# The feed-forward part of an encoder layer in two halves of channels, with a token-stationary up projection

## The chip, the cores and the metric

The kernel runs on one core of one Trainium2 chip. The metric is the device time of one execution in microseconds: 1326.75 us as the median of three runs of the kernel before. A core has five engines that run side by side and wait for each other through semaphores: TensorE (PE, matrix products), VectorE (DVE), ScalarE (ACT), GpSimd (POOL) and SyncE (SP, which issues most transfers). Matrix products write into eight banks of PSUM, from which DVE and ACT fetch them.

## The reference

One layer over 256 tokens of width 2048: a token mixer, then the part that is changed here, a convolutional gated MLP with 5504 channels, then a last norm. All inputs are float32.

```python
def conv_ffn(x, g_norm, w_up, conv_k, conv_b, w_down):
    h = rms_norm(x, g_norm)
    up = h @ w_up                                  # (256, 2048) @ (2048, 11008)
    t = up.shape[1]
    pad = jnp.pad(up, ((0, 0), (1, 1), (0, 0)))
    up = (pad[:, :t] * conv_k[0] + pad[:, 1:t + 1] * conv_k[1]
          + pad[:, 2:t + 2] * conv_k[2] + conv_b)  # width 3, over the tokens
    gate, val = jnp.split(up, 2, axis=-1)
    return x + (jax.nn.silu(gate) * val) @ w_down  # (256, 5504) @ (5504, 2048)
```

## The kernel before

Every product of two float32 matrices is done as three products of a rounded type: each operand is split into a high part and a low part, and high x high, low x high and high x low are added up in PSUM. Weights come from memory in pieces (tile `wraw`, five buffers). ACT writes the high part of a piece (`whi`, line 142), DVE the low part (`wlo`, line 143), both with four buffers. The function `begin(i)`, called ahead of piece i's products, issues the loads five pieces ahead, emits the split three pieces ahead, and then runs the tasks that other functions have hung on this step with `at(i, f)`. The program is emitted in exactly this order, and each engine works through its own list in order: what stands behind a waiting instruction waits as well. In the text a step is such an i.

There are two ways to multiply. In the weight-stationary one (`stationary`, `spread_products`, lines 194 and 198) a 128 x 128 block of weights is the stationary operand. The high part of the weights meets 512 columns, 256 tokens of the high and 256 of the low activations, and the low part of the weights meets the 256 high ones. In the token-stationary one (`wide`, `run_wide`, `triple`, lines 272 to 274) 128 tokens are stationary and 512 columns of weights move; one row block k of the weights, 2 x 512 columns wide, takes four triples of products (two token halves, two column halves). There, two neighbouring row blocks (a tile pair, a "quad" in the code) can be multiplied as a 2 x 2 block product with seven triples in place of eight. For this DVE forms sums of the activations (`act_sums`, lines 279 to 291, with a high part on ACT) and sums of the weights (`weight_sums`, lines 297 to 300; high and low parts in lines 307 and 308), and at the end sums of the results. In its own step i a tile pair has its activation sums made at i - 5 and i - 4, its weight sums at i - 3 and their parts at i - 2.

The feed-forward part before: the up projection is weight-stationary, in 22 groups of two channel blocks (the last of one) for gate and value each. After a group ACT and DVE add the two column halves (lines 936 and 938), multiply by the reciprocal of the norm (`rb`, line 944), convolve with three taps (lines 946 to 951), gate (lines 956 and 957) and split the result into `a` (lines 467 and 468). All 43 channel blocks are kept in SBUF. Then the down projection is token-stationary in two passes of 43 row blocks and 1024 columns each, with seven tile pairs in each pass:

```python
DOWN_QUADS = ((4, 6, 9, 11, 14, 16, 18), (3, 5, 8, 10, 13, 15, 17))
```

Its first pass is added to the residual `x2` while the second runs (`ev_down`, line 971); the second ends column half by column half (`finish`), with the last norm and the output.

## Time and profile before

| | |
|---|---|
| runs | 1326.64, 1326.75, 1327.16 us |
| profiled execution | 1326.71 us, span of its instructions 1324.7 us |
| TensorE busy | 1312.2 us (99%), granted clock 0.998 |
| VectorE busy | 1033.1 us (78%) |
| ScalarE busy | 763.7 us (58%) |
| up projection on TensorE | 605.74 to 1090.32 us of the span |
| down projection on TensorE | 1090.32 to about 1315.4 us |
| memory traffic | 253.90 MB read, 193 GB/s over the span |

The page lists each engine's busy time and the chain of work that ended last. The trace behind it also answers with lists of instructions in order of time (start, duration, engine, line, operation, tiles, count), with busy times of chosen stretches, with groups of equal instructions, and with sums of waits. In a product's name the moving operand stands first and the stationary one second. Durations of products overlap, so the pace of a stream is the distance between starts. Where several equal instructions are merged into a row, its duration runs from the first's start to the last's end.

### The profile page before, as it was taken

To read this page: it belongs to the slowest core of one execution; us is meant where nothing else is said; L and a number is where in the kernel's file an instruction comes from. 1 tells how busy PE (TensorE), PEld (TensorE's weight loads), DVE (VectorE), ACT (ScalarE), POOL (GpSimd) and SP (SyncE) were. 2 spreads that over 40 slices of the span, in tenths; PEclk is the share of its full clock that TensorE was granted. 3 is DMA by queue.
4 is the path that set the end of the run, shared out by engine and by line. 5 is a ranking of instruction groups with operands and counts; after the bars stand their busy time and mean duration, and the time that the engine had idled before them with its cause. 6 is when DMAs were issued, how large, how long until landed. Compare 5 with 4: busy or idle time off the path is not lost.

```text
span 1324.7 us, 19275 instructions
## 1 busy us (share of the span) xinstructions
PE 1312.2 (99%) x6791; PEld 1113.9 (84%) x6791; DVE 1033.1 (78%) x1561; ACT 763.7 (58%) x1127; POOL 105.0 (8%) x192
## 2 busy tenths in 40 slices
PE   9999999999999999999999999999999999999997
PEld 7888888888887888888888888888888888888885
DVE  6477667767598966986777778787878779999997
ACT  6665566667554644556655555565656556555553
POOL 0251145530000000000000000000000000000000
PEclk9999999999999999999999999999999999999999
DMA  9765785654656666665566665666666656656653
GB/s 329 228 182 182 212 225 171 210 175 154 198 173 209 202 195 224 218 208 175 175 192 190 182 194 183 190 182 192 183 191 191 191 148 234 215 192 207 213 197 121
DMA packets 174800, 259.37 MB, mean 196 GB/s; under 512 B 12920, under 2 KB 124400, under 8 KB 174704
## 3 DMA queue, kind: packets, MB, share of 16 engines
q1 hardware_dynamic: 170416, 250.31, 59.5%
q0 software_dynamic: 3968, 7.30, 2.2%
q8 instruction: 53, 0.87, 0.3%
q10 hardware_dynamic: 320, 0.53, 0.1%
q14 instruction: 43, 0.35, 0.1%
HBM read 253.90 MB, written 2.10 MB: 193 GB/s over the span
## 4 chain that ended last, share of the span: by engine, by line
PE 98%; DVE 1%; DMA 0%; ACT 0%; issue 0%; SPq 0%; ACTq 0%; DVEq 0%
PE bank L194 31%; PE bank L198 16%; PE bank L274 10%; PE bank L272 10%; PE bank L273 10%; PE bank L215 7%; PE bank L216 7%; PE bank L217 7%; PE bank L710 1%; DMA wraw<-in_w_in_dram 0%; PE bank L760 0%; PE bank L586 0%; PE bank L921 0%; PE bank L750 0%; PE bank L485 0%
## 5 line engine op out<-in xcount | busy, mean ns | idle before, releaser
L143 DVE TENSOR_TENSOR wlo<-wraw,whi 128x1024 fp32r<-128x1024 f32 (+1 forms) x471 | 554.2, 1186 | 216.9 <-ACT whi L142 205.4
L142 ACT ACTIVATE whi<-wraw 128x1024 fp32r<-128x1024 f32 (+1 forms) x471 | 477.3, 1026 | 297.3 <-PE bank L194 114.1
L194 PE MATMUL bank<-h,whi 128*128 128x512 f32 x1760 | 479.5, 395 | 0.0
L194 PEld LDWEIGHTS bank<-h,whi 128*128 128x128 f32 x1760 | 301.9, 189 | 41.5
L198 PEld LDWEIGHTS bank<-h,wlo 128*128 128x128 f32 x1760 | 267.3, 189 | 35.6
L198 PE MATMUL bank<-h,wlo 128*128 128x256 f32 x1760 | 276.7, 281 | 0.0
L215 PE MATMUL bank<-whi,h 128*128 128x512 f32 x256 | 102.2, 399 | 0.2 <-ACT whi L142 0.2
L274 PE MATMUL bank<-wlo,a 128*128 128x512 f32 x260 | 101.4, 390 | 0.2 <-DVE wlo L143 0.2
L272 PE MATMUL bank<-whi,a 128*128 128x512 f32 x260 | 101.2, 389 | 0.0
L273 PE MATMUL bank<-whi,a 128*128 128x512 f32 x260 | 101.2, 389 | 0.0
L216 PE MATMUL bank<-whi,h 128*128 128x512 f32 x256 | 100.1, 391 | 0.6 <-DVE h L464 0.6
L217 PE MATMUL bank<-wlo,h 128*128 128x512 f32 x256 | 100.1, 391 | 0.0
L946 ACT ACTIVATE tc<-ta,ck 128x256 f32<-128x256 f32 x86 | 47.3, 597 | 69.8 <-DVE ta L944 69.8
L274 PEld LDWEIGHTS bank<-wlo,a 128*128 128x128 f32 x260 | 48.8, 188 | 11.0 <-DVE wlo L143 1.0
L1222 POOL DMA_DIRECT2D gfin<-in_norm_final_dram x4 | 2.2, 550 | 700.2 <-DVE tc L957 580.4
L272 PEld LDWEIGHTS bank<-whi,a 128*128 128x128 f32 x260 | 48.8, 188 | 10.1
L273 PEld LDWEIGHTS bank<-whi,a 128*128 128x128 f32 x260 | 48.8, 188 | 10.1
L216 PEld LDWEIGHTS bank<-whi,h 128*128 128x128 f32 x256 | 48.1, 188 | 10.7 <-DVE h L464 1.4
L217 PEld LDWEIGHTS bank<-wlo,h 128*128 128x128 f32 x256 | 48.0, 188 | 10.7 <-DVE wlo L143 0.4
L215 PEld LDWEIGHTS bank<-whi,h 128*128 128x128 f32 x256 | 48.1, 188 | 10.1 <-ACT whi L142 0.6
L949 DVE SCALAR_TENSOR_TENSOR tc<-ta,ck,tc 128x255 f32<-128x255 f32 x86 | 41.4, 482 | 14.5 <-ACT tc L946 14.5
L215 PE MATMUL bank<-whi,y 128*128 128x512 f32 x128 | 50.4, 394 | 0.0
(254 smaller groups left out, 1684.8 us busy)
## 6 DMA issues: line engine op xcount, KB each, us to landing
wraw<-in_w_up_dram SPq DMA_DIRECT2D x336, 256.0 KB, 3.2
wraw<-in_w_in_dram SPq DMA_DIRECT2D x111, 512.0 KB, 4.0
wraw<-in_w_down_dram SPq DMA_DIRECT2D x86, 512.0 KB, 4.7
wraw<-in_w_in_dram SPq DMA_DIRECT2D x66, 256.0 KB, 3.8
wraw<-in_w_branch_dram SPq DMA_DIRECT2D x32, 512.0 KB, 3.8
wraw<-in_w_out_dram SPq DMA_DIRECT2D x32, 512.0 KB, 3.7
xs<-in_x_dram SPq DMA_DIRECT2D x8, 256.0 KB, 7.3
vw<-va POOLq DMA_DIRECT2D x32, 64.0 KB, 4.9
```

The costliest lines, as they stand in the source:

```text
L142: nc.scalar.activation(h[:, k, :m], w[:, k, :m], AF.Copy)
L143: nc.vector.tensor_sub(l[:, k, :m], w[:, k, :m], h[:, k, :m].bitcast(F32))
L194: nc.tensor.matmul(p, h[:, k - k0, b * 128:(b + 1) * 128], acts(k), start=k == 0, stop=k == nk - 1)
L198: nc.tensor.matmul(p[:, :T], l[:, k - k0, b * 128:(b + 1) * 128], acts(k)[:, 0, :], start=False, stop=False)
L215: nc.tensor.matmul(p, xh, h[:, kk, :m], start=st, stop=False)
L216: nc.tensor.matmul(p, xl, h[:, kk, :m], start=False, stop=False)
L217: nc.tensor.matmul(p, xh, l[:, kk, :m], start=False, stop=sp)
L272: nc.tensor.matmul(p, xh, h, start=st, stop=False)
L273: nc.tensor.matmul(p, xl, h, start=False, stop=False)
L274: nc.tensor.matmul(p, xh, l, start=False, stop=sp)
L946: nc.scalar.activation(v, u, AF.Identity, scale=ck[:, 1, ch:ch + 1], bias=ck[:, 3, ch:ch + 1])
L949: nc.vector.scalar_tensor_tensor(v[:, 1:], u[:, :T - 1], ck[:, 0, ch:ch + 1], v[:, 1:], op0=OP.mult, op1=OP.add)
```

## The change

The 43 channel blocks are cut into a first half of 20 and a second of 23. Each half does its up projection and then its share of the down projection, so that the down projection has four passes: two of 20 row blocks and two of 23. The first three are added to the residual from PSUM (`ev_part`, `ev_down`), the last ends as before.

The up projection becomes token-stationary, in groups of four channel blocks (the last of three) for gate and value: a piece of weights is one row block of 2 x 512 columns, gate and value, in one transfer. Pairs 3 and 5 of the eight row block pairs of a group are done with seven block products, except in the last group. The activations' sums for these two pairs are made once and used by all groups. The result now has tokens on the partitions. It is gathered in two tiles, `xa` and `xb` (first the sums of the seven products, then the plain products are added), and each channel block is then turned on TensorE: a product of 128 x 128 with the block as stationary operand and, as moving operand, a diagonal matrix with the reciprocal norm of the tokens (`rb`), for gate and value and both token halves. ACT copies the turned block from PSUM (`u`, three buffers). The multiplication by the norm on DVE goes. The taps, the gate and the split of a block are now spread over five steps (`conv`). The tiles for the sums lie in a pool of their own, since the activations `h` must last until the second half. The tile pairs of the down projection are 2 and 3 in the first half, 3 and 4 in the second.

```diff
@@ -45,7 +45,12 @@
 OUT_QUADS = ((3, 5), (1, 3))
 OUT_ORDER = (tuple(range(16)), (0, 1, 6, 7, 2, 3, 10, 11, 4, 5, 8, 9, 12, 13, 14, 15))
 TURN_X2 = (13, 1)
-DOWN_QUADS = ((4, 6, 9, 11, 14, 16, 18), (3, 5, 8, 10, 13, 15, 17))
+FFN_CUT = 20
+UP_QUADS = (3, 5)
+UP_TURN = (2, 3, 4, 5)
+UP_CONV = ((4, 7, 10, 13), (4, 6, 8, 10))
+DOWN_QUADS = (((5, 7), (2, 4, 6)), ((5, 7, 9), (2, 4, 6, 8)))
+ROOM_OF = {"f": "t13", "s": "xb"}
 
 
 @with_exitstack
...
-    def wide(src, row0, order, c0, acts, quads, room, done, sums=None):
-        n0 = plan_wide(src, row0, order, c0)
+    def wide(src, row0, order, c0, acts, quads, room, done, sums, pair=None, cn=512, step=512):
+        n0 = plan_wide(src, row0, order, c0, cn, step)
...
-                sum_acts_at(i - 5, i - 4, b["acts"], lambda k=order[2 * q]: ff["ap"][k // 2], room, "s")
+                sum_acts_at(i - 5, i - 4, b["acts"], lambda k=order[2 * q]: pair(k // 2), room, "s")
...
-            triple(C[t][c], x_of(order[i - n0], t), h[:, c], l[:, c], i == n0, i == n1 - 1)
+            triple(C[t][c][:, :cn], x_of(order[i - n0], t), h[:, c, :cn], l[:, c, :cn], i == n0, i == n1 - 1)
...
         s = const.tile([128, NT], F32, name="ss2")
         nc.vector.tensor_reduce(s, rs["ss"], axis=AX.X, op=OP.add)
         r = rstd("n2", s, D, RMS_EPS)
-        at(cur[0] + 3, lambda: rs.__setitem__("rb", bcast_cols(r)))
+        d = const.tile([128, T], F32, name="rb")
+        for t in range(NT):
+            nc.vector.tensor_scalar(d[:, t * 128:(t + 1) * 128], ident, r[:, t:t + 1], None, op0=OP.mult)
+        rs["diag"] = d
 
     def turn_x2(j):
         x2 = rs["x2"]
...
                                         x2[:, t, c * 128:(c + 1) * 128], ident)
             k = j * 4 + k2 * 2
             rs["h", k], rs["h", k + 1] = new_pair(hpool, f"h{k // 2}")
+            rs["hp", k // 2] = pair_of[hpool, f"h{k // 2}"]
             split_pair(p, (rs["h", k], rs["h", k + 1]), gffn[:, k:k + 2])
 
 
     ff = {}
 
-    def ev_up(f0, nb):
+    def ffn_room(name, dt):
+        return ff["room"].tile([128, 2, 512], dt, name=ROOM_OF.get(name, name))
+
+    def up_tiles():
+        x = [ffn_room(n, F32) for n in ("xa", "xb")]
+        ff["x"] = [[x[t][:, c] for c in range(2)] for t in range(NT)]
+
+    def ev_up_sums(P, i):
+        def go():
+            up_tiles()
+            p1, p5, p6, p7 = P
+            (x11, x12), (x21, x22) = ff["x"]
+            nc.scalar.activation(x11, p1, AF.Copy)
+            nc.vector.tensor_add(junk, p6, x11)
+            nc.vector.tensor_add(x12, p5, junk)
+            nc.vector.tensor_add(x21, p7, junk)
+            nc.vector.tensor_add(x22, p5, x21)
+
+        at(i + 1, go)
+
+    def ev_up(f0, a0, nb, summed, last):
         def done(ps, i):
-            n = nb
-            a = []
-            for p in ps:
-                t = tmp.tile([128, T], F32, name="tb", bufs=3)
-                nc.scalar.activation(t, p[:, T:], AF.Copy)
-                u = tmp.tile([128, T], F32, name="ta", bufs=6)
-                nc.vector.tensor_add(u, p[:, :T], t)
-                a.append(u)
+            m = nb * 128
+            if not summed:
+                up_tiles()
+            x = ff["x"]
+            for t in range(NT):
+                for c in range(2):
+                    v = x[t][c][:, :m]
+                    if summed:
+                        nc.vector.tensor_add(v, ps[t][c], v)
+                    elif c:
+                        nc.vector.tensor_copy(v, ps[t][c][:, :m])
+                    else:
+                        nc.scalar.activation(v, ps[t][c][:, :m], AF.Copy)
+            u = {}
+
+            def turn(b):
+                p = bank()
+                for c in range(2):
+                    for t in range(NT):
+                        nc.tensor.matmul(p[:, c * T + t * 128:c * T + (t + 1) * 128],
+                                         x[t][c][:, b * 128:(b + 1) * 128],
+                                         rs["diag"][:, t * 128:(t + 1) * 128], start=True, stop=True)
+                u[b] = ff["room"].tile([128, 2, T], F32, name="u", bufs=3)
+                nc.scalar.activation(u[b].rearrange("p a b -> p (a b)"), p, AF.Copy)
 
             def conv(b):
-                c = []
-                for u, ch in ((a[b], f0 + b), (a[n + b], NF + f0 + b)):
-                    nc.vector.tensor_mul(u, u, rs["rb"])
-                    v = ff["p"].tile([128, T], F32, name="tc", bufs=4)
-                    nc.scalar.activation(v, u, AF.Identity, scale=ck[:, 1, ch:ch + 1], bias=ck[:, 3, ch:ch + 1])
-                    c.append((u, v, ch))
-                for u, v, ch in c:
-                    nc.vector.scalar_tensor_tensor(v[:, 1:], u[:, :T - 1], ck[:, 0, ch:ch + 1], v[:, 1:],
-                                                   op0=OP.mult, op1=OP.add)
-                    nc.vector.scalar_tensor_tensor(v[:, :T - 1], u[:, 1:], ck[:, 2, ch:ch + 1], v[:, :T - 1],
-                                                   op0=OP.mult, op1=OP.add)
-                at(cur[0] + 1, lambda: gate(b, c[0][1], c[1][1]))
-
-            def gate(b, g, v):
-                nc.scalar.activation(g, g, AF.Silu)
-                nc.vector.tensor_mul(g, g, v)
-                at(cur[0] + 1, lambda: split_plain(g, ff["a"][f0 + b]))
-
-            at(i + 1, lambda: conv(0))
-            if n > 1:
-                at(i + (5 if f0 + 3 == NF else 3), lambda: conv(1))
+                j = cur[0]
+                v = [tmp.tile([128, T], F32, name="ta", bufs=6) for _ in range(2)]
+                chs = [c * NF + f0 + b for c in range(2)]
+
+                def taps():
+                    for c, ch in enumerate(chs):
+                        nc.vector.scalar_tensor_tensor(v[c][:, 1:], u[b][:, c, :T - 1], ck[:, 0, ch:ch + 1], v[c][:, 1:],
+                                                       op0=OP.mult, op1=OP.add)
+                        nc.vector.scalar_tensor_tensor(v[c][:, :T - 1], u[b][:, c, 1:], ck[:, 2, ch:ch + 1],
+                                                       v[c][:, :T - 1], op0=OP.mult, op1=OP.add)
+
+                y = ff["a"][a0 + b]
+                for c, ch in enumerate(chs):
+                    nc.scalar.activation(v[c], u[b][:, c], AF.Identity, scale=ck[:, 1, ch:ch + 1],
+                                         bias=ck[:, 3, ch:ch + 1])
+                at(j + 1, taps)
+                at(j + 2, lambda: nc.scalar.activation(v[0], v[0], AF.Silu))
+                at(j + 3, lambda: nc.vector.tensor_mul(v[0], v[0], v[1]))
+                at(j + 4, lambda: nc.scalar.activation(y[:, 0, :], v[0], AF.Copy))
+                at(j + 5, lambda: nc.vector.tensor_sub(y[:, 1, :], v[0], y[:, 0, :].bitcast(F32)))
+
+            for b in range(nb):
+                at(i + UP_TURN[b], lambda b=b: turn(b))
+                at(i + UP_CONV[last][b], lambda b=b: conv(b))
         return done
...
+    def ev_part(g):
+        def done(ps, i):
+            for j in range(2):
+                for t in range(NT):
+                    add_down(ps[t][j], t, 2 * g + j)
+        return done
...
-    g_up = []
-    for f in range(0, NF, 2):
-        nb = min(2, NF - f)
-        g_up.append(stationary(w_u, 0, KD, f * 128, nb * 128, 2, DFF, lambda k: rs["h", k], ev_up(f, nb)))
-    h_room = {n: f"h{i}" for i, n in enumerate(("t13", "t24", "h13", "h24", "l13", "l24", "f", "s"))}
-
-    def down_room(name, dt):
-        return hpool.tile([128, 2, 512], dt, name=h_room[name])
-
-    g_dn = [wide(w_d, 0, range(NF), g * 1024, lambda k: ff["a"][k], DOWN_QUADS[g], down_room,
-                 (ev_sums(2 * g, down_room), ev_down if g == 0 else finish)) for g in range(2)]
+    h_sums = {2 * q: {} for q in UP_QUADS}
+    halves = []
+    for f0, f1 in ((0, FFN_CUT), (FFN_CUT, NF)):
+        ups = []
+        for f in range(f0, f1, 4):
+            nb = min(4, f1 - f)
+            quads = UP_QUADS if nb == 4 else ()
+            ups.append(wide(w_u, 0, range(KD), f * 128, lambda k: rs["h", k], quads, ffn_room,
+                            (ev_up_sums, ev_up(f, f - f0, nb, bool(quads), f + 4 >= f1)), h_sums, cn=nb * 128, step=DFF))
+        downs = [wide(w_d, f0 * 128, range(f1 - f0), g * 1024, lambda k: ff["a"][k], DOWN_QUADS[len(halves)][g], ffn_room,
+                      (ev_sums(2 * g, ffn_room), ev_part(g) if not halves else finish if g else ev_down), None,
+                      lambda q: ff["ap"][q]) for g in range(2)]
+        halves.append((f1 - f0, ups, downs))
+    for n, q in enumerate(UP_QUADS):
+        i = halves[0][1][0][1] + 1 + 3 * n
+        sum_acts_at(i, i + 1, h_sums[2 * q], lambda q=q: rs["hp", q], ffn_room, f"s{n}")
 
 
     preload[0] = [lambda: load_x(0, 256)]
...
-    for g in g_up:
-        run_group(g)
...
-    run_wide(g_dn[0])
-    run_wide(g_dn[1], SPLIT_AHEAD + 1)
...
+    for n, ups, downs in halves:
+        ff["ap"] = [fa.tile([128, min(2, n - k), 2, T], F32R, name=f"a{k // 2}") for k in range(0, n, 2)]
+        ff["a"] = [ff["ap"][k // 2][:, k % 2] for k in range(n)]
+        for g in ups:
+            run_wide(g)
+        run_wide(downs[0])
+        run_wide(downs[1], SPLIT_AHEAD + 1 if downs is halves[1][2] else 0)
```

How this moves instructions, at three places. First TensorE in the up projection, before: the end of one group of two channel blocks and the start of the next (`h_5971` and `h_5762` are pairs of activations, `whi` and `wlo` the parts of the weights).

```order
L194 MATMUL bank<-h_5971,whi 128x512 x4
L198 MATMUL bank<-h_5971,wlo 128x256 x8
L194 MATMUL bank<-h_5971,whi 128x512 x4
L194 MATMUL bank<-h_5762,whi 128x512 x4
L198 MATMUL bank<-h_5762,wlo 128x256 x4
```

There each block of weights is loaded once for a product of 512 columns and its low part once for one of 256; nothing but such products stands there.

And of the change: the end of the group's second step, a turned block, and the start of its third step.

```order
L277 MATMUL bank<-whi,h_5760 128x512
L278 MATMUL bank<-whi,h_5760 128x512
L279 MATMUL bank<-wlo,h_5760 128x512
L980 MATMUL bank<-rb,xa 128x128
L980 MATMUL bank<-rb,xb 128x128
L980 MATMUL bank<-rb,xa 128x128
L980 MATMUL bank<-rb,xb 128x128
L277 MATMUL bank<-whi,h_5770 128x512
L278 MATMUL bank<-whi,h_5770 128x512
L279 MATMUL bank<-wlo,h_5770 128x512
```

The four products of L980 are new and stand between two steps of the next group, ahead of each of its steps 2 to 5 (counted from 0); the products around them have gone from blocks of weights as stationary operand to tokens.

Second, DVE in the first pass of the down projection, before: from the activation sums of the second tile pair to the weight sums (h6 the sums, h0 and h1 the weights' sums, h7 the low part of the activation sums).

```order
L279 TENSOR_TENSOR h6_11123<-a6_5863 128x512
L281 TENSOR_TENSOR h6_11123<-h6_11123 128x128
L282 TENSOR_TENSOR h6_11123<-h6_11123 128x128
L283 TENSOR_TENSOR h6_11123<-h6_11123 128x128
L284 TENSOR_TENSOR h6_11123<-h6_11123 128x128
L143 TENSOR_TENSOR wlo_11144<-wraw_11117,whi_11143 128x1024
L291 TENSOR_TENSOR h7_11147<-h6_11123,h7_11147 128x512
L143 TENSOR_TENSOR wlo_11166<-wraw_11141,whi_11165 128x512
L297 TENSOR_TENSOR h0_11169<-wraw_11141 128x512
L298 TENSOR_TENSOR h1_11170<-wraw_11163,h0_11169 128x512
L299 TENSOR_TENSOR h0_11169<-wraw_11163,wraw_11141 128x512
L300 TENSOR_TENSOR h1_11170<-wraw_11163,h1_11170 128x512
```

What stands there is the two pairs' sums and the low parts of weights alone.

Third, the same place of the change, in the first half: from the activation sums of its second tile pair to its weight sums (`ta` are the convolved blocks, `a8` the split result, `u` the turned blocks).

```order
L1006 TENSOR_TENSOR a8_5865<-ta_7989,a8_5865 128x256
L1004 TENSOR_TENSOR ta_8056<-ta_8056,ta_8057 128x256
L993 SCALAR_TENSOR_TENSOR ta_8116<-u_7998,ck_87,ta_8116 128x255
L995 SCALAR_TENSOR_TENSOR ta_8116<-u_7998,ck_87,ta_8116 128x255
L993 SCALAR_TENSOR_TENSOR ta_8117<-u_7998,ck_87,ta_8117 128x255
L995 SCALAR_TENSOR_TENSOR ta_8117<-u_7998,ck_87,ta_8117 128x255
L148 TENSOR_TENSOR wlo_8167<-wraw_8134,whi_8166 128x1024
L296 TENSOR_TENSOR xb_8170<-t13_8140,xb_8170 128x512
L148 TENSOR_TENSOR wlo_8195<-wraw_8164,whi_8194 128x512
L302 TENSOR_TENSOR t13_8198<-wraw_8164 128x512
L303 TENSOR_TENSOR t24_8199<-wraw_8192,t13_8198 128x512
L304 TENSOR_TENSOR t13_8198<-wraw_8192,wraw_8164 128x512
```

Between the sums of the second tile pair now stand the split of one block (L1006), the gate of the next (L1004) and the taps of a third (L993 and L995), which belong to the up projection's last group.

46 lines of the change are left out of this document (18 added, 28 removed).

## The prediction

> **What bounds the kernel now.** I read the page's totals and its chain first, then what TensorE (PE) waited for, then the stages.
>
> ```profile
> PE 1312.2 (99%) x6791; PEld 1113.9 (84%) x6791; DVE 1033.1 (78%) x1561; ACT 763.7 (58%) x1127; POOL 105.0 (8%) x192
> PE 98%; DVE 1%; DMA 0%; ACT 0%; issue 0%; SPq 0%; ACTq 0%; DVEq 0%
> ```
>
> The waits of PE, longest first (total, times, longest), begin with this row, and two stretches of 45 and 22 us of the up and the down projection read so (busy PE, weight loads, DVE, ACT, POOL; granted clock; DMA share, GB/s):
>
> ```profile
> PE bank L422 <- POOL ident masks.py:199: 1.4, 1, 1.4
> ```
>
> ```profile
> 765.00:810.00 45.00, 45.00 (x258) 39.37 (x257) 34.77 (x57) 26.16 (x42) 0.00 (x0) 1.00 0.61 188
> 1228.00:1250.00 22.00, 22.00 (x99) 18.22 (x98) 21.34 (x30) 13.04 (x15) 0.00 (x0) 1.00 0.65 220
> ```
>
> The longest wait of PE in the whole span is 1.4 us, at the start. In both stretches PE never stops, at clock 1.00, so the end moves by what is added to or taken from PE's stream, as long as the others keep up. They have unequal room: DVE is busy 77% of the up stretch and 97% of the down stretch, ACT 58% and 59%.
>
> A busy PE says nothing of its pace, since recorded matmuls overlap. I therefore price by distances between starts.
>
> ```profile
> 605.74 1.07 PE L194 MATMUL bank<-h,whi 128*128 128x512 f32 x4
> ...
> 608.52 1.04 PE L921 MATMUL bank<-ident,x 128*128 128x128 f32 x8
> 609.31 1.17 PE L194 MATMUL bank<-h,whi 128*128 128x512 f32 x4
> 610.32 0.64 PE L198 MATMUL bank<-h,wlo 128*128 128x256 f32 x4
> 610.79 1.09 PE L194 MATMUL bank<-h,whi 128*128 128x512 f32 x4
> 611.72 0.64 PE L198 MATMUL bank<-h,wlo 128*128 128x256 f32 x4
> ...
> 629.91 0.61 PE L449 MATMUL bank<-ident,n_r 128*128 128x128 f32 x4
> 630.27 1.17 PE L194 MATMUL bank<-h,whi 128*128 128x512 f32 x4
> ...
> 1090.32 0.39 PE L272 MATMUL bank<-whi,a 128*128 128x512 f32 x1
> ```
>
> The up projection runs from 605.74 to 1090.32, 484.6 us. Within it stand two sets of eight transposes (L921), which stay, 0.87 us each with the slower restart behind them (609.31 - 608.52 = 0.79, then 1.01 instead of 0.93), and the broadcast of the norm (L449), 630.27 - 629.91 = 0.36 and the same slower restart, 0.44 us. The products take 484.6 - 1.7 - 0.4 = 482.4 us for 86 blocks x 16 = 1376 pairs, 0.351 us a pair. A 512-column product costs 0.93/4 = 0.232 us, a 256-column one 0.47/4 = 0.118.
>
> ```profile
> 1194.82 0.39 PE L274 MATMUL bank<-wlo,a 128*128 128x512 f32 x1
> ...
> 1209.78 0.39 PE L274 MATMUL bank<-wlo,a 128*128 128x512 f32 x1
> ```
>
> In the token-stationary form of the down projection 66 products of 512 columns lie between these starts: 14.96/66 = 0.2267 us each.
>
> **The change, part by part. Products.** A pair held 512 + 256 columns for one block and one k; in the new form eight blocks and one k are 12 products of 512 columns, the same 6144 columns. Ten groups of four channel blocks have 16 x 4 = 64 triples, less one for each of their two tile pairs: 62. That is 10 x 62 x 3 x 0.2267 = 421.7 us. The last group has three blocks, no tile pair and 64 x 3 = 192 products of 384 columns; halfway between 0.118 and 0.2267 I take 0.172, 33.0 us. Together 454.7 us, 27.7 less than 482.4: 20 x 0.68 = 13.6 from the seven block products, the other 14.1 from pace.
>
> **The turn.** Each of 43 blocks now needs four products of 128 columns, a block of sums as stationary and the diagonal with the norm as moving operand, both plain float32. The nearest rows are the gMLP's mix, which has just this form and type, and the transposes within a 512-column stream:
>
> ```profile
> L586 PE MATMUL bank<-wsT,vg x32: 271/275/275, 88.4 to 122.3; 128*128 128x128 f32 x32
> 87.93 0.63 PE L198 MATMUL bank<-h,wlo 128*128 128x256 f32 x4
> 88.40 0.61 PE L586 MATMUL bank<-wsT,vg 128*128 128x128 f32 x4
> 88.77 1.17 PE L194 MATMUL bank<-h,whi 128*128 128x512 f32 x4
> 89.77 0.64 PE L198 MATMUL bank<-h,wlo 128*128 128x256 f32 x4
> 595.79 1.03 PE L921 MATMUL bank<-ident,x 128*128 128x128 f32 x8
> 596.58 0.48 PE L272 MATMUL bank<-whi,m 128*128 128x512 f32 x1
> 596.90 0.40 PE L273 MATMUL bank<-whi,m 128*128 128x512 f32 x1
> ```
>
> The kernel writes two products per group of the mix, 16 in all; the trace holds 32. So a float32 product runs as two passes, and a turn is eight. Four passes cost 88.77 - 88.40 = 0.37 and a restart 0.07 longer; eight would be 0.37 x 2 + 0.07 = 0.81 us. The eight transposes cost 596.90 - 595.79 - 0.23 = 0.88. I take 0.88, as its neighbours are the 512-column ones: 43 x 0.88 = 37.8 us, with 34.8 as the low end. So the turn eats more than the products give.
>
> [...]
>
> **Down projection.** Fourteen tile pairs become 2 + 3 + 3 + 4 = 12: two triples more, 1.4 us. The broadcast goes: -0.4. PE's sum: -27.7 + 37.8 + 1.4 - 0.4 = +11.1 us. Against the profiled execution's 1326.71 us (span 1324.7; the median of the runs, 1326.75, is the same) this gives 1337.8.
>
> **What must hide beside it.** Per up group DVE now does the following, priced by distances between starts:
>
> ```profile
> 710.99 0.42 DVE L468 TENSOR_TENSOR a<-tc,a 128x256 fp32r<-128x256 f32 x1
> 711.32 1.22 DVE L143 TENSOR_TENSOR wlo<-wraw,whi 128x1024 fp32r<-128x1024 f32 x1
> 703.52 0.48 DVE L949 SCALAR_TENSOR_TENSOR tc<-ta,ck,tc 128x255 f32<-128x255 f32 x1 [0.34 <-ACT tc L946]
> 705.36 1.22 DVE L143 TENSOR_TENSOR wlo<-wraw,whi 128x1024 fp32r<-128x1024 f32 x1
> 1202.02 2.48 DVE L971 TENSOR_TENSOR x<-bank,x 128x512 f32<-128x512 f32 x4
> 1204.41 1.22 DVE L143 TENSOR_TENSOR wlo<-wraw,whi 128x1024 fp32r<-128x1024 f32 x1
> 1235.24 0.69 DVE L279 TENSOR_TENSOR h<-a 128x512 f32<-128x512 f32 x1
> 1236.90 1.22 DVE L143 TENSOR_TENSOR wlo<-wraw,whi 128x1024 fp32r<-128x1024 f32 x1
> 1238.04 0.69 DVE L291 TENSOR_TENSOR h<-h,h 128x512 fp32r<-128x512 f32 x1
> 1238.64 0.69 DVE L143 TENSOR_TENSOR wlo<-wraw,whi 128x512 fp32r<-128x512 f32 x1
> 1239.24 0.69 DVE L297 TENSOR_TENSOR h<-wraw 128x512 f32<-128x512 f32 x1
> 1241.78 1.22 DVE L143 TENSOR_TENSOR wlo<-wraw,whi 128x1024 fp32r<-128x1024 f32 x1
> 1242.91 2.35 DVE L308 TENSOR_TENSOR h<-h,h 128x1024 fp32r<-128x1024 f32 x2
> 1245.18 1.22 DVE L143 TENSOR_TENSOR wlo<-wraw,whi 128x1024 fp32r<-128x1024 f32 x1
> 1246.32 0.69 DVE L279 TENSOR_TENSOR h<-a 128x512 f32<-128x512 f32 x1
> ```
>
> A low part of 1024 elements takes 1.14, of 512 0.60, a 256-element operation 0.33, the four taps of a block 1.84, four additions from PSUM 2.4 (some 2.7 where one needs the last). For a tile pair: sums of the activations 1.66 and their low part 0.60, sums of the weights 2.54 and their low parts 2.27. An up group: 14 x 1.14 + 2 x 0.60 + 2 x (2.54 + 2.27) + 2.7 + 2.4 + 4 x (1.84 + 2 x 0.33) = 41.9 us, against 42.2 + 3.5 = 45.7 us of PE. That hides: at 92% DVE is below the 97% with which the down stretch ran without a PE wait. ACT's new copy of each turned block goes into its idle 42%; the four passes over the residual instead of two add 2 x 12 additions of 0.60 on DVE, 14.4 us, and the two pairs fewer take 2 x 7.1 off. The up loads become one transfer of 512 KB for two of 256 KB, at the same bytes; the 188 GB/s above carry them, and if not, DVE's low parts are late by what a transfer is.
>
> The down projection does not hide so well. A step, one row block of weights, is 12 products, 2.72 us of PE; a tile pair shortens its two steps by 0.68 together. From 1235.24 to 1246.32 the trace shows a whole period of a pair every four steps: 11.1 us of DVE against 4 x 2.72 - 0.68 = 10.2 of PE. Each such pair makes DVE 0.9 us later, and the low parts are made three steps ahead (two for a pair's second block), a cover of 5.4 us. Before, three such pairs in a row were the most, and longer gaps followed. Now runs of pairs every four steps fill both second passes, and the first pass of each half lies on the tail of the convolutions. In half one's first pass, from step 5 up to the low part that step 14 needs, DVE has six low parts of 1024 and two of 512 (8.0), for its two pairs 2 x (1.66 + 0.60 + 2.54) + 2.27 = 11.9, the taps of four blocks (7.4) and five operations of 256 (1.6): 28.9 us. PE has 9 x 2.72 - 0.68 + 0.88 = 24.7 in steps 5 to 13, and 1.1 us more in step 14 before the product that uses it: 3.1 us of waiting, with the rest of the down projection queued behind that product on PE. The same sums give, as estimates, 1.7 us for its second pass, 3.4 for the first pass of half two (three pairs, three blocks) and 5.6 for the last (four pairs, and 2.4 + 2.4 of additions and scaling). Together 13.8; for the passes before, they give none, as PE's waits show. DVE may start a pair's low part a step sooner than I count, so I take 12, between 0 and 23. Forecast: 1337.8 + 12 = **1350 us**, 1.8% slower.
>
> **The rivals.** *PE's sum alone* (DVE's lateness stays under its cover): 1338, up to 1342. For it: PE waited nowhere in the passes before, at 97% DVE. Against it: the 28.9 against 24.7.
>
> *DVE bounds the up groups too.* Then the recorded durations, not the distances, count:
>
> ```profile
> L143 DVE TENSOR_TENSOR wlo<-wraw,whi 128x1024 fp32r<-128x1024 f32 x437 | 531.2, 1225 | 208.4 <-ACT whi L142 200.2 <-PE bank L849 3.0 <-DMA wraw<-in_w_in_dram 2.3
> ```
>
> By them (1.225 here; 0.69 for 512 elements, 0.48 a tap and 0.42 for 256 in the rows above) a group is 45.5 us, level with PE, and any wait on ACT is lost: at step 5 the fourth turned block's copy on ACT must wait for the first one's taps, since there are three buffers, and the next high part stands behind it, some 1.6 us. Ten groups: +16, 1366. Against it: in the rows above the next operation starts 0.09 us before the recorded end. [...]
>
> *The turn is cheap*, the other sign: its weight loads run under the preceding 512-column products, and only columns count. From 0.2267 and 0.118, a column costs 0.000425 us and 128 of them, with the same fixed part, 0.064: 344 passes x 0.064 = 22.0 us, 15.8 less. Without DVE waits 1322, faster by 0.4%; it decides below 0.078 us a pass, where 344 passes take less than 37.8 - 11.1 = 26.7 us. Against it: eight transposes in that very stream cost 0.11 each.
>
> *The seven-product form brings nothing* because its sums come late: at step 6 their low parts, made at step 4, have 3 steps' cover against 3.4 us of DVE work. It would return 13.6 us and end at 1363; I count it to the second rival.
>
> **Numbers.** Forecast with DVE late in the down passes 54%, PE's sum alone 27%, DVE bound throughout 10%, cheap turn 6%, and 3% for a cheap turn paid back by waits, near no change. The last two leave faster at 6%, within 0.2% (what a measurement here can tell from none) 3%, slower 91%. The range from 1337 to 1361 holds the first two cases whole; its ends are the sum with no wait and with some 23 us.
>
> **What would show it.** Right: L980 with 344 records at about 0.11 us a pass; up groups of 45.7 us on PE; waits of PE on DVE's low part (L148) only in the four down passes, 2 to 6 us in each, the last the longest. Wrong: passes under 0.08 us, PE waits within up groups, or none at all. A time under 1330 would overthrow the price of the turn, one above 1363 the DVE distances.

## The result, and the profile after

The changed kernel takes 1361.49 us (median of four runs, 1361.00 to 1361.69) against 1326.72 us (1326.64 to 1327.16) for the kernel before on the same chip: a ratio of 1.0261, 95% interval 1.0243 to 1.0279. The forecast of 1350 us had the sign right and was 11.5 us short; the time lies 0.5 us above the range. The profiled execution has a span of 1359.9 us.

The totals and the chain of the page after:

```profile
PE 1333.7 (98%) x6437; PEld 1118.1 (82%) x6437; DVE 1107.5 (81%) x1605; ACT 784.8 (58%) x1133; POOL 103.8 (8%) x190
PE 89%; DVE 8%; issue 1%; ACT 1%; DMA 0%; DVEq 0%; ACTq 0%
```

The chain was 98% PE and 1% DVE before; DVE's 8% are new. Stretches after: about one up group, most of the first pass of the down projection, then the middle of its third pass and most of its last (length; busy PE, weight loads, DVE, ACT, POOL; granted clock; DMA share, GB/s):

```profile
748.00:794.00 46.00, 46.00 (x223) 38.70 (x222) 41.94 (x61) 28.28 (x41) 0.00 (x0) 1.00 0.58 183
834.00:890.00 56.00, 50.17 (x228) 40.92 (x227) 47.55 (x76) 30.90 (x46) 0.00 (x0) 0.97 0.47 159
1250.00:1282.00 32.00, 29.13 (x120) 23.31 (x119) 31.72 (x46) 16.80 (x21) 0.00 (x0) 0.95 0.55 182
1282.00:1345.00 63.00, 57.63 (x241) 46.67 (x241) 61.54 (x91) 33.34 (x44) 0.00 (x0) 0.95 0.41 142
```

In the up group PE never stops. In the third and the last down pass DVE is busy 99 and 98% (31.72 of 32, 61.54 of 63) and PE 91%; in the first pass DVE has gaps (47.55 of 56, 85%), and still PE stands at 90%. Before, PE stood at 100% in the stretch shown of the down projection. The mean granted clock of these stretches falls to 0.95 to 0.97.

The turn and the group in the order of time on PE: a turn with its neighbours, then the first product behind the first turn of three successive groups.

```profile
655.57 0.38 PE L980 MATMUL bank<-rb,xa 128*128 128x128 f32 x2
...
656.37 0.48 PE L277 MATMUL bank<-whi,h 128*128 128x512 f32 x1
656.69 0.40 PE L278 MATMUL bank<-whi,h 128*128 128x512 f32 x1
...
702.62 0.48 PE L277 MATMUL bank<-whi,h 128*128 128x512 f32 x1
...
748.43 0.48 PE L277 MATMUL bank<-whi,h 128*128 128x512 f32 x1
...
794.21 0.48 PE L277 MATMUL bank<-whi,h 128*128 128x512 f32 x1
```

A turn is 656.37 - 655.57 = 0.80 and 0.09 of slower restart (0.32 in place of 0.23), 0.89 us; 0.88 was forecast. A group is 748.43 - 702.62 = 45.81 and 794.21 - 748.43 = 45.78 us; 45.7 was forecast.

PE's waits after in one row (total, times, longest), and then all seven in the order of time, the longest with the product ahead of it, and the last product of the kernel:

```profile
PE bank L279 <- DVE wlo L148: 14.1, 7, 3.6
```

```profile
866.45 0.50 PE L279 MATMUL bank<-wlo,a 128*128 128x512 f32 x1 [0.58 <-DVE wlo L148]
875.16 0.50 PE L279 MATMUL bank<-wlo,a 128*128 128x512 f32 x1 [1.61 <-DVE wlo L148]
878.50 0.39 PE L278 MATMUL bank<-whi,a 128*128 128x512 f32 x1
882.53 0.50 PE L279 MATMUL bank<-wlo,a 128*128 128x512 f32 x1 [3.64 <-DVE wlo L148]
1252.77 0.50 PE L279 MATMUL bank<-wlo,a 128*128 128x512 f32 x1 [1.02 <-DVE wlo L148]
1258.31 0.50 PE L279 MATMUL bank<-wlo,a 128*128 128x512 f32 x1 [1.85 <-DVE wlo L148]
1307.88 0.80 PE L279 MATMUL bank<-wlo,a 128*128 128x512 f32 x1 [3.42 <-DVE wlo L148]
1342.10 0.50 PE L279 MATMUL bank<-wlo,a 128*128 128x512 f32 x1 [1.95 <-DVE wlo L148]
1350.41 0.39 PE L279 MATMUL bank<-wlo,a 128*128 128x512 f32 x1
```

All of them are for a low part of the down weights. By distances between starts each is 0.16 longer than recorded (882.53 - 878.50 - 0.23 = 3.80 for 3.64): 6.3 us in the first pass, none in the second, 3.2 in the third, 5.7 in the last, 15.2 in all. Behind the last product (1350.41) lies a tail of 9.5 us.

Three of these waits have something behind them that was not forecast. PE after the wait that ends at 1307.88, and the reading of that stretch (columns as above, the granted clock third from the end):

```profile
1308.47 0.63 PE L277 MATMUL bank<-whi,xb 128*128 128x512 f32 x1
...
1313.16 0.63 PE L279 MATMUL bank<-l,xb 128*128 128x512 f32 x1
1313.59 0.47 PE L277 MATMUL bank<-h,a 128*128 128x512 f32 x1
```

```profile
1308.47:1313.59 5.12, 5.12 (x13) 3.96 (x12) 5.05 (x9) 0.34 (x1) 0.00 (x0) 0.50 0.56 192
```

Twelve products start 0.427 us apart (1313.59 - 1308.47 = 5.12) instead of 0.227, at a granted clock of 0.50. In the whole kernel there are 27 such products, 7, 1, 7 and 12 in the four passes: 5.4 us.

So the 23.7 us between the sum of PE's work that was forecast (1337.8) and the time are 15.2 of waits, 5.4 of half pace, and 3.1 left for PE's own work and for the single products of 0.3 us that stand at the edges of waits.

### The profile page after: what moved, and what is told of

The parts are those of the page before. It is cut to its first block, busy times and chain, and to the rows that moved or that the text cites. A ratio compares the mean times of both kernels' runs of the same rounds, so it can differ in the third digit from the quotient of the medians.

```text
span 1359.9 us, 18277 instructions
## 1 busy us (share of the span) xinstructions
PE 1333.7 (98%) x6437; PEld 1118.1 (82%) x6437; DVE 1107.5 (81%) x1605; ACT 784.8 (58%) x1133; POOL 103.8 (8%) x190
## 4 chain that ended last, share of the span: by engine, by line
PE 89%; DVE 8%; issue 1%; ACT 1%; DMA 0%; DVEq 0%; ACTq 0%
PE bank L279 18%; PE bank L277 18%; PE bank L278 18%; PE bank L199 7%; PE bank L220 7%; PE bank L221 6%; PE bank L222 6%; PE bank L203 3%; PE bank L980 3%; DVE wlo L148 2%; DVE l L313 1%; PE bank L715 1%; DVE t L303 0%; DVE t L302 0%; PE bank L765 0%
## 5 line engine op out<-in xcount | busy, mean ns | idle before, releaser
L148 DVE TENSOR_TENSOR wlo<-wraw,whi 128x1024 fp32r<-128x1024 f32 (+2 forms) x471 | 542.9, 1163 | 208.6 <-ACT whi L147 194.1
L147 ACT ACTIVATE whi<-wraw 128x1024 fp32r<-128x1024 f32 (+2 forms) x471 | 467.6, 1006 | 290.1 <-PE bank L278 149.2
L277 PE MATMUL bank<-whi,h 128*128 128x512 f32 (+1 forms) x676 | 262.8, 389 | 0.0
L278 PE MATMUL bank<-whi,h 128*128 128x512 f32 (+1 forms) x676 | 259.7, 384 | 0.0
L279 PE MATMUL bank<-wlo,h 128*128 128x512 f32 (+1 forms) x676 | 259.6, 384 | 0.0
L279 PEld LDWEIGHTS bank<-wlo,h 128*128 128x128 f32 x676 | 126.9, 188 | 23.9
L277 PEld LDWEIGHTS bank<-whi,h 128*128 128x128 f32 x676 | 127.0, 188 | 22.8
L278 PEld LDWEIGHTS bank<-whi,h 128*128 128x128 f32 x676 | 127.1, 188 | 22.8
L279 PE MATMUL bank<-wlo,a 128*128 128x512 f32 x272 | 107.1, 394 | 14.1 <-DVE wlo L148 14.1
L199 PE MATMUL bank<-h,whi 128*128 128x512 f32 x384 | 106.0, 398 | 0.0
L313 DVE TENSOR_TENSOR l<-t,h 128x1024 fp32r<-128x1024 f32 x84 | 98.9, 1218 | 0.0
L279 PEld LDWEIGHTS bank<-wlo,a 128*128 128x128 f32 x272 | 51.1, 188 | 28.0 <-DVE wlo L148 17.5
L199 PEld LDWEIGHTS bank<-h,whi 128*128 128x128 f32 x384 | 65.8, 189 | 9.1
L203 PEld LDWEIGHTS bank<-h,wlo 128*128 128x128 f32 x384 | 58.0, 189 | 7.6
L203 PE MATMUL bank<-h,wlo 128*128 128x256 f32 x384 | 60.1, 281 | 0.0
```

What stands on the lines that cost most here:

```text
L147: nc.scalar.activation(h[:, k, :m], w[:, k, :m], AF.Copy)
L148: nc.vector.tensor_sub(l[:, k, :m], w[:, k, :m], h[:, k, :m].bitcast(F32))
L199: nc.tensor.matmul(p, h[:, k - k0, b * 128:(b + 1) * 128], acts(k), start=k == 0, stop=k == nk - 1)
L203: nc.tensor.matmul(p[:, :T], l[:, k - k0, b * 128:(b + 1) * 128], acts(k)[:, 0, :], start=False, stop=False)
L277: nc.tensor.matmul(p, xh, h, start=st, stop=False)
L278: nc.tensor.matmul(p, xl, h, start=False, stop=False)
```

## The experiments

Labels are those on record. All are edits of the changed kernel, and every time stands beside runs of the kernel before on the same chip (1326.6 to 1327.0 us).

**Fewer tile pairs in the down projection.** Nine instead of twelve, and mostly further apart.

```diff
-DOWN_QUADS = (((5, 7), (2, 4, 6)), ((5, 7, 9), (2, 4, 6, 8)))
+DOWN_QUADS = (((7,), (2, 5, 7)), ((7, 9), (3, 6, 8)))
```

> The changed kernel with nine tile pairs in the down projection in place of twelve: 7; 2, 5, 7 in the first half, 7, 9; 3, 6, 8 in the second, all at least five steps apart or clear of the convolutions. Three triples more on TensorE, +2.0 us. Theory: the 34.8 us are the sum of TensorE's stream (some 12), its waits for DVE's low parts in three of the four down passes (starts 15 to 17 us late) and products at half pace behind the three longest waits (some 5.5, starts 0.43 us apart instead of 0.227). Without the crowding both of the last go: 1361.5 - 16.5 - 5.5 + 2.0 = about 1341, no wait for low parts above 0.5 us, clock 0.998 again. Rival, the waits only move (DVE's work is the same in the up groups and bounds them next): 1355 or more, with waits in the up groups. Rival, the slow clock has its own cause: 1347, with stretches at 0.43 us that follow no wait.

Measured: 1343.52 us, ratio 1.0126 (1.0109 to 1.0143). PE's waits in this kernel's trace:

```profile
PE bank L279 <- DVE wlo L148: 1.3, 1, 1.3
```

PE got three triples more (2.0 us) and the kernel became 18.0 us faster; no product runs at half pace. Less 2.0 and less the 1.4 of the wait left, PE's own sum with twelve pairs would be 1340.1. The lateness of DVE in the down passes costs 18.0 + 2.0 + 1.4 = 21.4 us by this run, not 12.

**The fourth turn of the last up group one step later.** Only the first half has one: the last group of the second half has three blocks. The copy of the fourth turned block (`u`, L984) needs the buffer of the first one, so it waits for that block's taps on DVE. Across the changed kernel this row of the groups shows it; the row under it, from ACT's order of time, is the instance in the first down pass, and the third, from DVE's, what DVE then waited for:

```profile
L984 ACT ACTIVATE u<-bank 128x512 f32<-128x512 f32 x43 | 25.3, 588 | 37.2 <-DVE ta L995 33.4 <-PE bank L980 3.5
```

```profile
855.97 0.60 ACT L984 ACTIVATE u<-bank 128x512 f32<-128x512 f32 x1 [4.86 <-DVE ta L995]
```

```profile
857.54 1.22 DVE L148 TENSOR_TENSOR wlo<-wraw,whi 128x1024 fp32r<-128x1024 f32 x1 [1.70 <-ACT whi L147]
```

```diff
-                at(i + UP_TURN[b], lambda b=b: turn(b))
+                at(i + UP_TURN[b] + (last and b == 3), lambda b=b: turn(b))
```

> The fourth turned block of each half's last up group one step later, so that its copy on ACT no longer waits for the taps of the first block (three buffers). In the trace of the change this copy waited 4.9 us in the first half's first down pass, the high part behind it was late and DVE stood idle 1.7 and 0.5 us. Theory: this is the part of that pass's lateness that the prediction left out; its waits fall from about 6.3 to about 4.2 us, the time by 2 to 3 us to about 1359. Rival (the lateness is DVE's own work alone, as priced): within 0.5 us of the change, 1361.5.

Measured: 1358.76 us, ratio 1.0241 (1.0226 to 1.0257), 2.7 us less. The same copy in this kernel, on ACT:

```profile
854.93 0.60 ACT L984 ACTIVATE u<-bank 128x512 f32<-128x512 f32 x1 [0.22 <-DVE ta L995]
```

The first two waits of the first down pass are gone with it. From the first product of the first half's down passes to the first of the next up group it is 948.61 - 832.73 = 115.88 us on PE, against 951.50 - 833.75 = 117.75 in the changed kernel: 1.9 us less. The rest of the 2.7 lies ahead of the up projection, which starts at 605.15 us here and at 606.18 there; the edit changes nothing in that part. So 1.9 us of DVE's lateness came from ACT, and the forecast had that wait in a rival only.

**The turn in one pass.** A transpose against the identity in place of the product with the diagonal; the norm's factor is put in at the evictions on DVE and, for the sums of the pairs, by a scaling on ACT.

```diff
-                        nc.tensor.matmul(p[...], x[t][c][...], rs["diag"][...], start=True, stop=True)
+                        nc.tensor.transpose(p[...], x[t][c][...], ident)
...
-                        nc.vector.tensor_add(v, ps[t][c], v)
+                        nc.vector.scalar_tensor_tensor(v, ps[t][c], r, v, op0=OP.mult, op1=OP.add)
...
+        at(i + 3, scale)
```

> The turn as a transpose with the identity, one pass in place of two, 172 passes instead of 344. The norm is multiplied in before: ACT scales the four sums of the seven products (four more operations of 512 per group), DVE scales the plain products while it adds them. Theory (a turn is priced by its passes, 0.11 us each): 172 x 0.11 = 18.9 us less, about 1342.5; the waits of the down passes stay as they are. Rival (the turn hides partly behind weight loads, so passes cost less than the distances say): 8 to 14 us less. Rival (DVE bounds the shorter up groups: 41.9 of 43.9 us): 5 to 10 us less, with new waits in the up groups.

Measured: 1360.23 us, ratio 1.0252 (1.0237 to 1.0267): 1.3 us less, not 19. PE's waits here, and two groups' turns 45.84 us apart:

```profile
PE bank L985 <- DVE xb L974: 9.7, 16, 1.0
```

```profile
746.60 0.33 PE L985 MATMUL bank<-ident,xa 128*128 128x128 f32 x1
747.91 0.33 PE L985 MATMUL bank<-ident,xb 128*128 128x128 f32 x1 [0.98 <-DVE xb L974]
...
792.44 0.33 PE L985 MATMUL bank<-ident,xa 128*128 128x128 f32 x1
```

The up group did not get shorter, because now DVE arrives late with the evictions. DVE's own list in such a group is hardly longer than before (only the form of four evictions changed, 0.74 us each in place of 0.68), but it holds a gap, here in this kernel's ACT and DVE rows:

```profile
763.28 0.60 ACT L988 ACTIVATE u<-bank 128x512 f32<-128x512 f32 x1 [3.20 <-DVE ta L999]
```

```profile
764.86 1.83 DVE L148 TENSOR_TENSOR wlo<-wraw,whi 128x1024 fp32r<-128x1024 f32 x2 [1.69 <-ACT whi L147]
```

The copy that waits for a buffer holds back the next high part on ACT, and DVE waits 1.7 us for that. While the turns took PE their full time, this gap cost nothing; with shorter turns it is to be expected that it does, and the next run tries that.

**One pass, with these gaps mended.** The fourth turn at step 6 in every group, and the scaling on ACT one step earlier.

```diff
-UP_TURN = (2, 3, 4, 5)
+UP_TURN = (2, 3, 4, 6)
...
-        at(i + 3, scale)
+        at(i + 2, scale)
```

> The turn as a plain transpose of one pass, the norm's factor put in by DVE's and ACT's evictions; unlike in e3_one_pass the scaling of the sums stands on ACT one step earlier, and the fourth block of a group is turned at step 6 instead of 5, so its copy on ACT no longer meets a buffer whose taps have not run. Theory (in e3 the groups stayed at 45.8 us because two waits, the buffer of the turned block and the scaling on ACT ahead of a high part, took away DVE's slack; DVE's own work is 42 us a group): groups of about 44.0 us on PE, 43 turns x 0.44 = 18.9 us less and 2.7 us less at the fourth turn of the last group: 1340 us, 1339 to 1344 with the down passes as late as before. Rival (DVE's recorded durations, not the distances, bound the group, whatever waits are taken away): groups stay at 45.5 to 45.8 us, 1356 to 1359.

Measured: 1347.73 us, ratio 1.0158 (1.0143 to 1.0173): 12.5 us less than e3_one_pass. Two groups apart on PE:

```profile
746.34 0.33 PE L985 MATMUL bank<-ident,xb 128*128 128x128 f32 x1 [0.22 <-DVE xb L974]
...
790.90 0.33 PE L985 MATMUL bank<-ident,xb 128*128 128x128 f32 x1 [0.22 <-DVE xb L974]
```

A group is 44.56 us. The rival (held at 45.5 to 45.8 whatever is taken away) falls. Two things were moved in this run, and which of them did how much was not separated. The expectation of 44.0 was not met either: the first turn of each group still meets DVE's last eviction.

**The same with nine tile pairs in the down projection**, as in the first experiment.

> As e7_one_pass_late, and with nine tile pairs instead of twelve in the down projection, as in e1_few_down_pairs. Theory: 1340 less the 18.0 us that this edit took in e1: 1322 to 1326, at or a little below the kernel before (1326.7). Rival (DVE bounds the up groups): 1338 to 1341.

Measured: 1329.99 us (nine runs), ratio 1.0025 (1.0016 to 1.0035): 17.7 us below e7_one_pass_late, where 18.0 had been measured for this edit alone. The two edits add up; the rest to the expectation of 1322 to 1326 is in the main again the up groups' half microsecond.

**No tile pairs in the up projection.**

```diff
-UP_QUADS = (3, 5)
+UP_QUADS = ()
```

> The changed kernel without tile pairs in the up projection: its ten full groups use 64 plain triples instead of 62. Theory (PE sets the pace in the up groups, DVE hides there): each group gets two triples of 0.68 us longer, 45.8 to 47.2 us, in all +13.6 us: 1375 us, with the four down passes as before. Rival (the sums for the pairs come late or cost as much as they save, so the seven block products bring nothing): within 2 us of the changed kernel, 1360 to 1363.

Measured: 1374.28 us, ratio 1.0362 (1.0346 to 1.0377): 12.8 us more. The seven block products of the up projection are worth nearly their full 13.6 us, and the rival that they bring nothing falls. A group's stretch in this kernel:

```profile
749.00:796.00 47.00, 47.00 (x225) 39.50 (x224) 30.16 (x42) 26.33 (x39) 0.00 (x0) 1.00 0.62 180
```

DVE has 36% to spare here, and still PE waits in the down passes (8 waits, 15.1 us recorded, against 7 and 14.1 in the changed kernel): the lateness does not come over from the up groups.

**The waits filled.** Products with a stationary block of zeros (which add nothing), meant to stand ahead of the three waits that are followed by half pace: 15, 8 and 15 of them.

```diff
+                for _ in range(fill.get(i, 0)):
+                    nc.tensor.matmul(C[0][0], zero, h1[:, 0], start=False, stop=False)
...
+    fill[halves[0][2][0][1] + 14] = 15
+    fill[halves[1][2][0][1] + 18] = 8
+    fill[halves[1][2][1][1] + 8] = 15
```

> The changed kernel with products of a stationary block of zeros put in just ahead of the three products that waited longest (15, 8 and 15 of 512 columns; they add zero): 3.4, 1.8 and 3.4 us of TensorE work inside waits of 3.8, 2.0 and 3.6 us. Nothing is taken away, and no wait is shortened. Theory (products run at half pace because TensorE stood idle before): the stretches with starts 0.43 us apart go, 1361.5 - 5 = about 1356.5. Rival (the slow stretches come from something else, such as the load itself): 1361.5 or a little more, stretches still there.

Measured: 1361.60 us, ratio 1.0262 (1.0246 to 1.0277), no change. PE's waits in this kernel (L355 is L279's part of the products with a fill), then the middle wait and the middle fill (L354):

```profile
PE bank L355 <- DVE wlo L148: 5.0, 7, 1.8
PE bank L279 <- DVE wlo L148: 4.6, 3, 2.0
```

```profile
1257.80 0.50 PE L355 MATMUL bank<-wlo,a 128*128 128x512 f32 x1 [1.84 <-DVE wlo L148]
...
1268.13 2.03 PE L354 MATMUL bank<-whi,zero 128*128 128x512 f32 x8
```

The two fills of 15 stand in their waits, from 878.19 and from 1304.03 us, and no half pace follows them. The fill of 8 missed: it stands one tile pair too late, at a place where PE waited for nothing in the changed kernel, so it is 1.8 us of added work, and the wait of 1.84 us it was meant for stayed empty. No half pace followed that wait either, though the same two waits, 1.0 and 1.8 us, are followed by it in the changed kernel.

The first half is a clean trial all the same. From the first product of its down passes to the first of the next up group PE takes 951.01 - 833.26 = 117.75 us, exactly as in the changed kernel (951.50 - 833.75). The eight slow products there (1.6 us) are gone, and in their place two new waits stand in the second pass, 0.55 and 0.58 us recorded, 1.45 together by the starts. What PE gained in pace it waited for DVE one pass later. My theory, that the half pace is a cost of its own beside the waits, falls for the first half. For the second half the run cannot tell: its down passes take 0.9 us longer (1350.83 - 1213.19 = 137.64 to the last product, against 1350.41 - 1213.69 = 136.72), with the stray fill of 1.8 us, two new waits of 0.76 and 0.57 us and eight products at half pace behind the last wait.

**DVE relieved alone.** For the plain row blocks of the down projection no low part is made; the product that would read it reads the high part again. That part of the sum is left out; the work of PE, ACT and the transfers stays.

```diff
+            if src is w_d and i not in units:
+                l = h
...
-                nc.vector.tensor_sub(l[:, k, :m], w[:, k, :m], h[:, k, :m].bitcast(F32))
+                if l is not h:
+                    nc.vector.tensor_sub(l[:, k, :m], w[:, k, :m], h[:, k, :m].bitcast(F32))
```

> The changed kernel, but for the plain row blocks of the down projection DVE makes no low part; the products that would read it read the high part again, so that part of the sum is wrong. PE's, ACT's and the DMA queues' work is unchanged, and so is the number of tile pairs; only DVE has 1.14 us less at each plain step of the down projection. Theory (in the down passes nothing but DVE's lateness costs time, the half-pace products behind the long waits included): all waits of PE there go and no product is slow, 1361.5 - 16.6 - 5.4 = 1339.5, 1338 to 1342. Rival (the tile pairs cost PE itself time, by their order or by the banks): above 1350.

Measured: 1344.41 us, ratio 1.0131 (1.0115 to 1.0148): 17.1 us less, with the same twelve tile pairs. PE's waits left here:

```profile
PE bank L283 <- DVE wlo L152: 3.6, 2, 2.5
```

Two waits, 3.9 us by the starts, and 8 products at half pace (1.6) remain, so not all waits went, and the time is 2.4 us above the expected 1338 to 1342. Without them it would be 1338.9. The tile pairs cost PE itself nothing that shows within some 1 us; DVE's work is what makes the difference.

**The last pass: one pair less, or its sums later.** Two edits that take the same last wait away, one by less work on DVE, one by another order.

```diff
-DOWN_QUADS = (((5, 7), (2, 4, 6)), ((5, 7, 9), (2, 4, 6, 8)))
+DOWN_QUADS = (((5, 7), (2, 4, 6)), ((5, 7, 9), (2, 4, 6)))
```

> The changed kernel; only the last pass of the down projection loses the fourth of its four tile pairs (at 8). PE gets one triple more, 0.7 us; DVE has about 7.1 us less in the second half of the pass. Theory (DVE's total from the start of the pass to the end of the kernel sets its length, waits only show where the lateness surfaces): the 8.3 us which this pass loses go but for 8.3 - 7.1 - 0.7 = 0.5: 1354 us, 1353 to 1356. Rival (what is lost at the wait for the second pair's sums, 3.6 us and the half-pace products behind it, is lost before the fourth pair matters; only the last wait of 2.1 us goes): 1360 us, 1359 to 1361.

Measured: 1359.88 us, ratio 1.0246 (1.0232 to 1.0260), as the rival said. This kernel's waits are the six others of the changed kernel:

```profile
PE bank L279 <- DVE wlo L148: 12.1, 6, 3.6
```

What is lost at the second pair's sums, 1304 to 1313 us, is lost there; slack that DVE gets afterwards does not bring it back.

```diff
-            at(i + 1, first_half)
-            at(i + 2, second_half)
+            at(i + 1 + late, first_half)
+            at(i + 2 + late, second_half)
```

(`late` is 1 in the last pass and 0 in the others.)

> The changed kernel; only in the last pass of the down projection the eight additions of the pair sums (L872 to L881, the first five 3.25 us by their starts) are issued one step later, behind the last low part of the weights instead of ahead of it. Theory (these additions, which the list of DVE's work for the last pass left out, are what makes the last low part late): the last wait of PE, 2.34 - 0.23 = 2.1 us, goes, and no other wait grows, 1359.4 us, 1358.9 to 1360. Rival (DVE's total decides the end whatever the order, since its additions must be done before the end): 1361.0 to 1361.8.

Measured: 1361.94 us, ratio 1.0262 (1.0247 to 1.0278): nothing, as the rival said. The last product on PE, and DVE's last addition of the pair sums and the next operation, in this kernel:

```profile
1348.04 0.39 PE L279 MATMUL bank<-wlo,a 128*128 128x512 f32 x1
```

```profile
1344.02 0.68 DVE L881 TENSOR_TENSOR x<-x,t 128x512 f32<-128x512 f32 x1
1344.62 0.69 DVE L1019 TENSOR_TENSOR x<-bank,x 128x512 f32<-128x512 f32 x1
```

The last wait did go (one of 0.35 us appeared at 1330.88) and PE ends earlier, but in a span of 1360.4 us the tail behind 1348.04 is 12.4 us instead of 9.5: the additions now stand between PE's last columns and the output. At the end of this kernel DVE's list decides, and moving work within it gained nothing.

**A version level with the kernel before.** First e8_one_pass_late_few with the first three turns a step later as well and the sums of the last pass later; then, once the run above had shown the tail, with the sums where the change has them and two pairs in the last pass. Two lines of the second, against the changed kernel (the turn is the one-pass turn of above):

```diff
-UP_TURN = (2, 3, 4, 5)
+UP_TURN = (3, 4, 5, 6)
...
-DOWN_QUADS = (((5, 7), (2, 4, 6)), ((5, 7, 9), (2, 4, 6, 8)))
+DOWN_QUADS = (((7,), (2, 5, 7)), ((7, 9), (3, 6)))
```

> As e8_one_pass_late_few, with the first three turns also one step later (steps 3, 4, 5, 6), so that the evictions on DVE are done before the first turn, and the pair sums of the last pass one step later as in e11. Theory: the waits ahead of the turns, 9 x 0.26 and once 1.1, and the last wait, 1.4, go: 1330.0 - 2.3 - 1.1 - 1.4 = 1325.2 us, 1324.5 to 1326.5, that is the kernel before (1326.6) or 0.1% below it. Rival (the turns and copies now fall together with the sums of the first pair, and DVE or ACT is late there): 1329 to 1334.

> As e10_all_mended, but the pair sums of the last pass stay where the change has them, and that pass has two tile pairs, at 3 and 6, instead of three. Theory (the last pass is bound by DVE to its end, so work taken off DVE there counts and work moved to the end does not): e10's last product starts at 1313.60; one triple more makes that 1314.3, and the tail behind it goes from 12.3 back to 9.5 us: a span of 1323.8 and, with 1 to 2 us around the span, 1325 to 1326, 0.1% below the kernel before. Rival (the tail stays long, or a new wait appears in the last pass): 1327 to 1329.

Measured: e10_all_mended 1327.01 us (eleven runs), ratio 1.0000 (0.9991 to 1.0009); its PE work ends at 1313.60 in a span of 1325.9, so the long tail (12.3 us, against 9.5 in e8_one_pass_late_few) took back 2.8 of the 4.6 us by which PE ended earlier (1318.17 there), and the expectation of 1325.2 was missed by 1.8. e12_mended_two_pairs 1325.20 us (eleven runs), ratio 0.9985 (0.9976 to 0.9994): 0.15% below the kernel before, 2.7% below the changed one. That is less than the 0.2% which the forecast took as what can be told from no change; with eleven runs the interval leaves 1 out by a little, and the slowest of them (1325.54) lies below the fastest of the fifteen of the kernel before (1326.36). Its waits of PE behind the start of the up projection, and one up group:

```profile
PE bank L277 <- ACT u L988: 0.5, 1, 0.5
```

```profile
746.00:790.00 44.00, 43.95 (x202) 36.03 (x201) 41.48 (x60) 30.72 (x45) 0.00 (x0) 1.00 0.63 187
```

## Why the prediction fell short, step by step

*Products and turn: right.* The group (45.8 for 45.7) and the turn (0.89 for 0.88, in 344 records) came out as worked out from the rows of before. The cheap turn, the rival on the other side, falls with the 0.80 us of eight passes, 0.10 each. PE's own sum was put at 1337.8; the runs give 1338.9 (DVE relieved), 1340.1 (nine pairs) and 1340.9 (waits and half pace subtracted): 1 to 3 us low. Of this 1.6 us lies in the up projection: its two stretches on PE, from first to first product, are 833.75 - 606.18 = 227.6 and 1213.69 - 951.50 = 262.2 us, 489.8 together, where the sum has 484.6 - 27.7 - 0.4 and 36 of the 43 turns (31.7; the other seven stand in the down passes), 488.2. In the down passes PE's own work came out as summed: 110.3 + 125.9 us in the run with nine pairs, less its three triples and its wait, is 232.7; the sum has 1315.18 - 1090.32 = 224.9 from the kernel before, 1.4 for two triples and 6.2 for seven turns, 232.5.

*DVE hides in the up groups: right, with little to spare.* No wait of PE above 0.2 us in any of them. The rival that DVE bounds them named the copy that waits for a buffer; the wait is there (33.4 us on ACT), but cost nothing in the groups until the turn was made shorter.

*DVE late in the down passes: the step that failed, by its size.* The passes were put at 3.1, 1.7, 3.4 and 5.6 us, 13.8 together, and I took 12. As waits they measured 6.3, 0, 3.2 and 5.7, and with the half-pace products 7.7, 0.2, 4.6 and 8.1, together 20.6. Two other ways give the same size: 18.0 + 2.0 + 1.4 = 21.4 by the run with nine pairs, 17.1 + 3.9 + 1.6 = 22.6 by the run without low parts. So the term was 21 to 23 us, not 12.

In the first half the traces show what was left out. Here are ACT's, PE's and DVE's rows of the changed kernel: the high part of a piece, PE's step 5 (its first row is the fourth turn), the low part of that piece, and the low part that the longest wait was for.

```profile
850.04 1.06 ACT L147 ACTIVATE whi<-wraw 128x1024 fp32r<-128x1024 f32 x1 [1.05 <-PE bank L278]
```

```profile
850.07 0.38 PE L980 MATMUL bank<-rb,xa 128*128 128x128 f32 x2
```

```profile
851.13 1.23 DVE L148 TENSOR_TENSOR wlo<-wraw,whi 128x1024 fp32r<-128x1024 f32 x1 [2.35 <-PE bank L980]
...
881.26 1.22 DVE L148 TENSOR_TENSOR wlo<-wraw,whi 128x1024 fp32r<-128x1024 f32 x1
```

DVE's list from step 5 to the low part for step 14 takes from 851.13 to 881.26 and 1.14 more, 31.3 us. In it are two waits for ACT, 1.70 us (shown with the second experiment) and 0.50; without them it is 29.1, and 28.9 was priced. So the list itself was right. Left out were the 2.2 us of waits and the start: the list begins 1.06 us behind PE's step 5, since the high part waits for PE to be done with an earlier piece, and the low part for the high part, which ends at 850.04 + 1.06 = 851.10. 3.1 + 2.2 + 1.1 = 6.4, and 6.3 was measured. The second pass was put at 1.7 us and shows no wait; with the first pass's wait filled, 1.45 us of waits do appear there. In the changed kernel PE came to that pass later by its slow products and so had nothing left to wait for. The text priced the ACT wait further on, for another rival, and did not add it here. Rounding 13.8 down to 12, because a low part might start a step sooner, had no row behind it; in the first pass it started later than counted.

In the second half the list gave 9.0 us, and 8.9 of waits and 3.8 of half pace were measured; this part is open in the main. One piece of it can be named. In the last pass stand the evictions of the pair sums ahead of the last late low part (DVE after, in order of time):

```profile
1337.58 0.68 DVE L872 TENSOR_TENSOR x<-bank,x 128x512 f32<-128x512 f32 x1
...
1340.83 1.22 DVE L148 TENSOR_TENSOR wlo<-wraw,whi 128x1024 fp32r<-128x1024 f32 x1
```

These are 3.25 us, and the prediction's list for that pass names only 2.4 + 2.4 of additions and scaling (its total for DVE has these sums, in the 2 x 12 additions). 5.6 + 3.2 = 8.8 would be near the 8.1 measured, but that is argued from the list: the run that moved them took the last wait away, and so did the run with one pair less, so the wait needs both, and the first could not price them, since the tail took the time back. That 5.6 us were forecast and 5.7 of waits measured in the last pass is therefore luck in part: 2.1 of the 5.7 are the wait that these sums helped to make.

*The seven block products bring nothing:* fell, with 12.8 of 13.6 us measured.

*What would show it:* L980, the groups and the place of the waits (the down passes only) were as written; "the last the longest" was not: the longest recorded wait, 3.64 us, is in the first pass, and the second pass of the first half, for which 2 to 6 us were expected as for the others, has none.

*The range* ended at 1361 as the sum with 23 us of lateness. The lateness stayed at or below that (20.6 to 22.6); the 1 to 3 us by which PE's own sum was low carried the time past it. The range left no room for that term.
